# HGRN2's values and K turned by VectorE and transfers, and retention's states weighted ahead of a sum by ones, from the third unit on

## The chip, the cores and the metric

One core of a Trainium2 chip runs one launch of the kernel. The metric is device time in microseconds (us), median of three executions. The profile is of one execution. Its engines are written PE (TensorE matmuls), PEld (TensorE weight loads), DVE (VectorE), ACT (ScalarE), POOL (GpSimd) and SP (the queue from which nearly all transfers are issued).

## The reference, cut to what matters

One decoder layer works on 16 meta tokens, 256 prompt tokens and 8 sample tokens (one new token of each of 8 sequences with a past state):

```python
x = layer_norm(ALPHA * x + 0.5 * swiglu_1(x))
x = layer_norm(ALPHA * x + mixer(x))
x = layer_norm(ALPHA * x + 0.5 * swiglu_2(x))

# mixer: ten projections of x, 2048 wide each; retention (8 heads of 256), HGRN2 (16 heads of 128)
o = inner @ v + (q * decay) @ S                   # of one sequence, chunk by chunk
S_new = decay_to_the_end * S + k_decayed.T @ v
# the 8 samples: one token each, on a state of their own (8 x heads x 256 x 256, 8 x 16 x 128 x 128)
y = sigmoid(a_r) * norm(o_ret) * silu(g_r) + sigmoid(a_h) * rms_norm(o_hg) * silu(g_h)
out = y @ w_out
```

Two sums of it are touched. The HGRN2 state needs `K.T @ v` over the tokens, so both K and the values must stand with tokens on the partitions, while the projections leave them with features there. And a retention sample's output is its query times its new state, a sum over 256 features: 8 samples and 2 halves of 128 features for each head.

## The kernel before, in words

Activations lie with features on partitions and 280 tokens (or 264, without the meta tokens) in the free dimension. Every weight block of 128 x 128 is split into an upper and a lower part (`whi`, `wlo`), every activation into `xh` and `xl`, and a block costs three matmuls (whi with xh, whi with xl, wlo with xh), all on line 218. Weights come in loads of 8 blocks (512 KB): SP issues the transfer into `raw`, ACT casts it to `whi` (line 188), DVE subtracts to `wlo` (line 189), and 24 matmuls use them. Each of the three tiles has three buffers, so a new `raw` transfer waits until the `wlo` of three loads before is made, and a new `whi` until the 24 matmuls of three loads before are done.

The middle stage handles eight units; a unit is one retention head and two HGRN2 heads. A unit has six projection groups (f, q_h, i_h, q_r, k_r, v_r) and then four gate groups of the unit before it (g_r with a_r, g_h with a_h, twice), ten groups of 16 steps; a step is 6 matmuls, two blocks. So a unit is 960 dense matmuls, or 40 weight loads. The mixers `mix_hg` and `mix_ret` are generators. `evacuate`, called when a group's sums are complete, starts them: `mix_hg` at the end of i_h, `mix_ret` at the end of v_r. After each step `pump` counts the generators down, and each `yield n` lets n steps pass before the next piece is put into the program. PE's order is that of the program, and the matmuls of the mixers stand between dense ones at steps that the yields set. The other engines and SP run queues in an order which a scheduler wrote from priorities and its own estimates when the program was built; each then waits at the head of its queue for semaphores. The first two units differ in some pauses; the last six are alike, and this text calls them the steady units.

What the change touches:

- `mix_hg`, values. `i_h` ends; ACT copies both heads from PSUM to `v` (lines 667 and 668). For each head PE turns two blocks of 128 tokens (`pt<-ident,v`, line 875), in the second head's step also `ends`, the meta tokens and the last 16 columns (line 878), and ACT copies the result to `vt` (tile `vth`).
- `mix_hg`, K. When K is scaled, `turned(h)` turns two blocks of each head on PE (`ptk<-ident,K`, line 982), one head at a time, and ACT copies them to `kth`. `pst` (lines 1022 and 1024) multiplies them with `vth` to the states `Sh`; `pq` (line 1039) is the samples' product; `po` the outputs.
- `mix_ret`, states. `load` brings the sample states (`smr`, four tiles of 128 x 4 x 256: two groups `e` of four samples, two halves `c` of the features), ACT scales them by the decay (line 1192), DVE adds key times value (line 1198, the value spread over partitions as `vbr`), SP writes them out (`out_srs`, line 1202). Later `pqr` (line 1211) multiplies 16 pieces, `smr[e][c][:, j, :]`, by `qdr`, a tile of zeros in which each sample's query stands in one column, 32 columns a piece, summed in PSUM.
- POOL has small copies only, some of which do nothing but hold a transfer back until a tile is free (lines 769 and 773).

Of the kernel before, what the change touches and what calls it, by code (L numbers as in the profile page):

```python
# [13 lines left out]
AF = mybir.ActivationFunctionType  # L14
# [4 lines left out]
P = 128  # L19
# [109 lines left out]
def trunk(ctx: ExitStack, tc: tile.TileContext, A, O):  # L129
# [417 lines left out]
    with tc.tile_pool(name="yp", bufs=1) as yp:  # L547
# [7 lines left out]
        with tc.tile_pool(name="mp", bufs=1) as mp:  # L555
# [35 lines left out]
            nc.gpsimd.memset(qdh, 0.0)  # L591
            nc.gpsimd.memset(qdr, 0.0)
            qdh_at = [qdh.rearrange("p a c -> p (a c)")[:, 256 * h :] for h in range(2)]
            qdr_at = [qdr.rearrange("p a c -> p (a c)")[:, 2 * ALONE * c :] for c in range(2)]
            vsm = tmp("vsm", (P, P))
            vt2 = tmp("vt2", (P, 2, P))
# [51 lines left out]
            def evacuate(n, c0, c1, o0, o1, b0, b1):  # L648
# [12 lines left out]
                        mul_biased(q[:, j, :], o, b, q[:, j, :])  # L661
                    st["q"] = q
                elif n == "i_h":
                    v = st.pop("i_h", None)
                    if v is None:
                        v = tmp("v", (P, 2, T))
                        nc.scalar.copy(v[:, 0, :], o0)
                        nc.scalar.copy(v[:, 1, :], o1)

                    start(mix_hg(c0 // 2, st["f"], st["k"], st["q"], v), {0: 20, 2: 46}.get(c0, 4))  # L670
                elif n in ("q_r", "k_r"):
                    sc, w, x0 = (1.0, TL, NMETA) if n == "q_r" else (KSC, T, 0)
                    r = tmp(n, (P, 2, w))
# [8 lines left out]
                elif n == "v_r":  # L682
                    v = tmp("v", (P, 2, T))
                    nc.scalar.copy(v[:, 0, :], o0)
                    nc.scalar.copy(v[:, 1, :], o1)
                    start(mix_ret(c0 // 2, st["q_r"], st["k_r"], v), 24 if c0 == 2 else 3)
                elif n in ("g_r", "g_h"):
                    sg = tmp("gs", (P, TL), bufs=2)
                    t = tmp("gt", (P, TL), bufs=2)
                    nc.scalar.activation(sg, o0, AF.Sigmoid)  # L690
                    mul(t, sg, o0)
                    sa = tmp("gs", (P, TL), bufs=2)
                    nc.scalar.activation(sa, o1, AF.Sigmoid)
                    mul(t, t, sa)
                    u, e = divmod(c0, 2)
                    while u not in (done_r if n == "g_r" else done_h):
                        pump()
                    if n == "g_r":
                        y = tmp("y", (P, TL))
                        mul(y, t, on_r[u][:, e, :])  # L700
                        st["y"] = y
                    else:
                        y = st["y"]
                        nc.vector.scalar_tensor_tensor(
                            out=t, in0=t, scalar=ngt[:, c0 : c0 + 1], in1=on_h[u][:, e, :], op0=ALU.mult, op1=ALU.mult)

                        ys[c0] = y if c0 < EARLY else yp.tile([P, TL], F32, tag=f"y{c0}", name=f"y{c0}")
                        add(ys[c0], y, t)
                        if c0 < EARLY:
                            split(yh[c0], yl[c0], y)  # L710

            NB2 = LP - 2 * P
            BLOCKS = ((0, P), (P, P), (2 * P, T - 2 * P))

# [6 lines left out]
            def upper_upper_lower(out, x, at=0):  # L721
                n = x.shape[0]
                nc.scalar.copy(out[:n], x)
                nc.scalar.copy(out[32 : 32 + n], x)
                sub(out[64 : 64 + n], x, out[at : at + n].bitcast(F32))

            def rows_out(src, width, tag):

# [17 lines left out]
            def mix_hg(u, f, k, q, v):  # L746

                calm = 2
                ends = tmp("ends", (P, 2, 2, NMETA))
                nc.gpsimd.tensor_copy(ends[:, :, 0, :], v[:, :, :NMETA])  # L750
                nc.gpsimd.tensor_copy(ends[:, :, 1, :], v[:, :, T - NMETA :])
# [114 lines left out]

                join(1)
                Q1 = side_by_side(1)
                vt = tmp("vth", (P, 2, 2, P))
                vrow = []  # L870
                for h in range(2):

                    pt = mx_bank("pt")
                    for b in range(2):
                        nc.tensor.transpose(pt[:, b * P : (b + 1) * P], v[:, h, NMETA + b * P : NMETA + (b + 1) * P], ident)
                    x = pt[:64, 2 * P : 3 * P]
                    if h:
                        nc.tensor.transpose(x, ends.rearrange("p c a t -> p (c a t)"), ident)
                    nc.scalar.copy(vt[:, h], pt[:, : 2 * P].rearrange("p (b f) -> p b f", b=2))
# [205 lines left out]
            def mix_ret(u, q, k, v):  # L1085
# [18 lines left out]
                for c in range(2):  # L1104
# [84 lines left out]
                for e in range(2):  # L1189
# [11 lines left out]
                    for c in range(2):  # L1201
                        nc.sync.dma_start(O["srs"][u, c, :, 4 * e : 4 * e + 4, :], ss[c])
                    yield 1 if e else 10 if u == 0 else 6
                yield (11 if u == 0 else 15) + 2 * calm
                pq = mx_bank("pqr")
                scores(pq[:, 256:], 2)
                for e in range(2):
                    for c in range(2):
                        for j in range(4):
                            b = 4 * e + j  # L1210
                            nc.tensor.matmul(  # L1211
                                pq[32 * j : 32 * j + 32, :256], qdr_at[c][:, 32 * b : 32 * b + 32],
                                sms[2 * e + c][:, j, :], start=e + c == 0, stop=e + c == 2, tile_position=(0, 32 * j))
# [163 lines left out]
```

## Time and profile before

| what | value |
|---|---|
| time, median of 3 | 2566.66 us (2566.41 to 2567.9) |
| the profiled execution, first to last instruction | 2563.9 us |
| what lies around the span, against the median | 2.8 us |
| busy: PE, PEld | 2553.4, 2534.4 us |
| busy: DVE, ACT, POOL | 1702.8, 1392.2, 57.0 us |
| granted TensorE clock | 1.000 |
| data moved | 536.26 MB, mean 209 GB/s |
| middle stage, a steady unit | 126.3 us |

The page gives the profiled execution's span, and no time of its own besides. An engine counts as busy while one of its instructions runs. Matmuls overlap, so a row of 280 ns for one matmul is not its cost: in the timeline the dense matmuls start 0.119 us apart with 280 columns and 0.1125 us apart with 264. What a piece of other PE work costs is read from how far it pushes the next dense matmul back.

### The profile page before, as it was taken

The numbers are of one execution on the slowest core, as the hardware profiler recorded it, in microseconds if no ns is written. First come the engines' busy times: TensorE is split into PE (matmuls) and PEld (weight loads), VectorE is DVE, ScalarE is ACT, GpSimd is POOL, SyncE is SP. The second block draws the span as 40 slices with busy tenths as digits, with TensorE's granted clock in tenths as the row PEclk, the third lists the DMA queues.
The fourth block names the chain that finished last, engine by engine and source line by source line (L and its number), as shares of the span: only waits on it lengthen the run. The fifth ranks groups of instructions, "written<-read, shape, count | busy, mean of one in ns | idle before, by whom it ended". The sixth has DMA issues, their size and how long they took to land.

```text
span 2563.9 us, 56275 instructions
## 1 busy us (share of the span) xinstructions
PE 2553.4 (100%) x23424; PEld 2534.4 (99%) x23424; DVE 1702.8 (66%) x2827; ACT 1392.2 (54%) x2186; POOL 57.0 (2%) x152
## 2 busy tenths in 40 slices
PE   9999999999999999999999999999999999999999
PEld 9999999999999999999999999999999999999998
DVE  6444544475569878777777777777885555556555
ACT  5444444444456767767676666675564444444443
POOL 0000000000000000000000000000000000000000
PEclk9999999999999999999999999999999999999999
DMA  7555555555555876767676767675556565565554
GB/s 244 183 187 183 187 182 184 186 182 186 184 201 180 287 265 232 264 214 260 212 264 215 259 223 255 224 239 188 196 190 197 194 197 195 194 196 195 195 195 149
DMA packets 156897, 536.26 MB, mean 209 GB/s; under 512 B 17952, under 2 KB 25952, under 8 KB 156640
## 3 DMA queue, kind: packets, MB, share of 16 engines
q1 hardware_dynamic: 156352, 532.37, 62.0%
q8 instruction: 183, 3.00, 0.5%
q14 instruction: 74, 0.61, 0.1%
q10 hardware_dynamic: 288, 0.29, 0.0%
HBM read 501.99 MB, written 30.61 MB: 208 GB/s over the span
## 4 chain that ended last, share of the span: by engine, by line
PE 96%; DVE 2%; ACT 0%; issue 0%; DMA 0%; SPq 0%; ACTq 0%; DVEq 0%
PE up L218 36%; PE dn L218 19%; PE pj_i_h L218 3%; PE pj_g_r L218 3%; PE pj_q_h L218 3%; PE pj_g_h L218 3%; PE pj_a_r L218 3%; PE pj_a_h L218 3%; PE pj_f L218 3%; PE pj_q_r L218 3%; PE pj_k_r L218 3%; PE wo L218 3%; PE pj_v_r L218 3%; DVE wlo L189 1%; PE pqr L1211 1%; PE psr L1168 0%
## 5 line engine op out<-in xcount | busy, mean ns | idle before, releaser
L189 DVE TENSOR_TENSOR wlo<-raw,whi 128x1024 fp32r<-128x1024 f32 (+1 forms) x869 | 1062.2, 1223 | 740.7 <-ACT whi L188 737.3
L188 ACT CAST whi<-raw 128x1024 fp32r<-128x1024 f32 (+1 forms) x870 | 905.7, 1042 | 909.2 <-PE up L218 411.0
L218 PE MATMUL up<-xh,whi 128*128 128x280 f32 (+1 forms) x2624 | 725.6, 280 | 0.6 <-ACT whi L188 0.6
L218 PE MATMUL up<-xh,wlo 128*128 128x280 f32 (+1 forms) x2624 | 725.8, 280 | 0.4 <-DVE wlo L189 0.3
L218 PE MATMUL up<-xl,whi 128*128 128x280 f32 (+1 forms) x2624 | 725.4, 279 | 0.0
L218 PEld LDWEIGHTS up<-xh,wlo 128*128 128x128 f32 x2624 | 492.6, 189 | 1.0 <-DVE wlo L189 1.0
L218 PEld LDWEIGHTS up<-xh,whi 128*128 128x128 f32 x2624 | 492.6, 189 | 0.8 <-ACT whi L188 0.8
L218 PEld LDWEIGHTS up<-xl,whi 128*128 128x128 f32 x2624 | 492.6, 189 | 0.0
L218 PE MATMUL dn<-hh,whi 128*128 128x280 f32 (+1 forms) x1376 | 384.7, 280 | 0.0
L218 PE MATMUL dn<-hh,wlo 128*128 128x280 f32 (+1 forms) x1376 | 384.3, 279 | 0.0
L218 PE MATMUL dn<-hl,whi 128*128 128x280 f32 (+1 forms) x1376 | 384.3, 279 | 0.0
L218 PEld LDWEIGHTS dn<-hh,whi 128*128 128x128 f32 x1376 | 260.1, 189 | 0.1
L218 PEld LDWEIGHTS dn<-hl,whi 128*128 128x128 f32 x1376 | 260.1, 189 | 0.1
L218 PEld LDWEIGHTS dn<-hh,wlo 128*128 128x128 f32 x1376 | 260.1, 189 | 0.0
L218 PE MATMUL pj_k_r<-xh,whi 128*128 128x280 f32 x256 | 74.2, 290 | 0.0
L218 PE MATMUL pj_g_r<-xh,whi 128*128 128x264 f32 x256 | 74.0, 289 | 0.0
L218 PE MATMUL pj_v_r<-xh,whi 128*128 128x280 f32 x256 | 73.8, 288 | 0.0
L218 PE MATMUL pj_v_r<-xh,wlo 128*128 128x280 f32 x256 | 72.4, 283 | 0.3 <-DVE wlo L189 0.3
L218 PE MATMUL pj_g_h<-xh,whi 128*128 128x264 f32 x256 | 72.7, 284 | 0.0
L218 PE MATMUL pj_k_r<-xh,wlo 128*128 128x280 f32 x256 | 72.4, 283 | 0.0
L218 PE MATMUL pj_v_r<-xl,whi 128*128 128x280 f32 x256 | 72.3, 283 | 0.0
L218 PE MATMUL pj_k_r<-xl,whi 128*128 128x280 f32 x256 | 72.3, 283 | 0.0
(421 smaller groups left out, 5263.4 us busy)
## 6 DMA issues: line engine op xcount, KB each, us to landing
raw<-in_w_up SPq DMA_DIRECT2D x343, 512.0 KB, 4.1
raw<-in_w_in SPq DMA_DIRECT2D x320, 512.0 KB, 4.3
raw<-in_w_dn SPq DMA_DIRECT2D x172, 512.0 KB, 3.5
smr<-in_sr SPq DMA_DIRECT2D x32, 512.0 KB, 5.0
out_srs<-smr SPq DMA_DIRECT2D x32, 512.0 KB, 6.7
raw<-in_w_out SPq DMA_DIRECT2D x32, 512.0 KB, 3.9
vbr<-vrd SPq DMA_DIRECT2D x32, 256.0 KB, 4.1
smh<-in_sg SPq DMA_DIRECT2D x16, 512.0 KB, 5.2
```

The lines of the kernel that those rows point to most:

```text
L188: nc.scalar.copy(hi[:, j:jn, :], raw[:, j:jn, :])
L189: nc.vector.tensor_tensor(out=lo[:, j0:j1, :], in0=raw[:, j0:j1, :], in1=hi[:, j0:j1, :].bitcast(F32), op=ALU.subtract)
L218: nc.tensor.matmul(o, w, t, start=start, stop=stop)
L1211: nc.tensor.matmul(pq[32 * j : 32 * j + 32, :256], qdr_at[c][:, 32 * b : 32 * b + 32], sms[2 * e + c][:, j, :], start=e + c == 0, stop=e + ...
```

## The change

For units with u > 1 alone:

- Values: DVE turns blocks of 32 x 32 straight from PSUM (two instructions on 128 x 256, into the tile `v`), and 16 transfers of SP put the blocks in their places in `vth` (`turned_over`, one transfer each second step). ACT copies only the end columns. PE keeps the turn of `ends`.
- K: one DVE instruction turns 128 x 512 into the tile `k` (which is no longer needed then), and 16 transfers put the blocks into the tile `f`, from which `pst` reads. POOL's copies that hold back transfers now read `k` and `f`.
- Pauses of `mix_hg`: 30 steps instead of 5 ahead of `pst`, 42 instead of 45 between `pst` and `pq`.
- Retention's samples: after the states went out they are weighted in place by the queries. POOL (for e = 0) or ACT (for e = 1) multiplies the half c = 0 by its query column, DVE multiplies the half c = 1 by its own and adds: 4 + 4 + 8 instructions on 128 x 256. A copy from the latest gate tile (`st["seen"]`) stands ahead of the queries' copy on POOL. `pqr` then needs 8 pieces instead of 16, with ones in a column in place of the queries.
- Pauses of `mix_ret`: a start after 5 steps instead of 3, and 23 + 16 steps instead of 19 ahead of `pqr`.

```diff
             qdh_at = [qdh.rearrange("p a c -> p (a c)")[:, 256 * h :] for h in range(2)]
+            one = qdr[:, 0, :64].rearrange("p (e m) -> p e m", e=2)
+            late_q = qdr[:, 1, : 2 * NS].rearrange("p (c b) -> p c b", c=2)
...
                 elif n == "i_h":
-                    v = st.pop("i_h", None)
-                    if v is None:
+                    v, vt = st.pop("i_h", None), tmp("vth", TURNED)
+                    ends = tmp("ends", (P, 2, 2, NMETA))
+                    if c0 > 2:
+                        z = squared(tmp("v", (P, 2, T)))
+                        for j, o in enumerate((o0, o1)):
+                            nc.vector.transpose(z[:, j].rearrange("p b t -> p (b t)"), o[:, NMETA:LP])
+                            nc.scalar.copy(ends[:, j, 0, :], o[:, :NMETA])
+                            nc.scalar.copy(ends[:, j, 1, :], o[:, T - NMETA : T])
+                        turned_over(vt, z, 2)
+                    elif v is None:
...
-                    start(mix_ret(c0 // 2, st["q_r"], st["k_r"], v), 24 if c0 == 2 else 3)
+                    start(mix_ret(c0 // 2, st["q_r"], st["k_r"], v), {0: 3, 2: 24}.get(c0, 5))
...
                     nc.scalar.activation(sa, o1, AF.Sigmoid)
+                    st["seen"] = sa
...
+            TURNED = (P, 2, 2, P)
+            squared = lambda x: x.rearrange("p h t -> p (h t)")[:, : 4 * P].rearrange("p (h b t) -> p h b t", h=2, b=2)
...
+            def turned_over(out, z, pause):
+
+                def transfers():
+                    for i in range(0, P, 32):
+                        for j in range(0, P, 32):
+                            nc.sync.dma_start(out[j : j + 32, :, :, i : i + 32], z[i : i + 32, :, :, j : j + 32])
+                            yield pause
+
+                start(transfers(), 1)
...
-                    nc.gpsimd.tensor_copy(sms[h][:, 0, :1], kts[0][:, 0, :1] if h else acc[:, 15:16])
+                    nc.gpsimd.tensor_copy(sms[h][:, 0, :1], (kts[0] if u < 2 else k)[:, 0, :1] if h else acc[:, 15:16])
...
-                    nc.gpsimd.tensor_copy(vbs[h][:, 0, :1], kts[1][:, 0, :1] if h else acc[:, 2 * P + 15 : 2 * P + 16])
+                    n = 32 if h and u > 1 else P
+                    nc.gpsimd.tensor_copy(vbs[h][:n, 0, :1], kts[1][:n, 0, :1] if h else acc[:, 2 * P + 15 : 2 * P + 16])
...
-                    pt = mx_bank("pt")
-                    for b in range(2):
-                        nc.tensor.transpose(pt[:, b * P : (b + 1) * P], v[:, h, NMETA + b * P : NMETA + (b + 1) * P], ident)
+                    if u < 2 or h:
+                        pt = mx_bank("pt")
+                    if u < 2:
+                        for b in range(2):
+                            nc.tensor.transpose(pt[:, b * P : (b + 1) * P], v[:, h, NMETA + b * P : NMETA + (b + 1) * P], ident)
...
-                kts = []
+                kts = [squared(f)[:, h] for h in range(2)] if u > 1 else []
 
                 def turned(h):
+                    if u > 1:
+                        if h == 0:
+                            z = squared(k)
+                            nc.vector.transpose(z.rearrange("p h b t -> p h (b t)"), K[:, :, NMETA:])
+                            turned_over(squared(f), z, 2)
+                        return
...
                     samples(1)
-                    yield 4 if u == 0 else 5
+                    yield 4 if u == 0 else 30
...
-                yield (8, 11, 45)[min(u, 2)]
+                yield (8, 11, 42)[min(u, 2)]
...
-                alone(qdr, q)
+                if u < 2:
+                    alone(qdr, q)
...
-                yield (11 if u == 0 else 15) + 2 * calm
+                yield (11, 15, 13)[min(u, 2)] + 2 * calm if u < 2 else 23
+                if u == 2:
+                    nc.gpsimd.memset(qdr[:, 0, :64], 0.0)
+                    for e in range(2):
+                        nc.gpsimd.memset(one[:, e, e : e + 1], 1.0)
+                if u > 1:
+                    nc.gpsimd.tensor_copy(late_q[:, 0, :1], st["seen"][:, :1])
+                    nc.gpsimd.tensor_copy(late_q, q[:, :, SEQ:])
+                    for e in range(2):
+                        s0, s1 = sms[2 * e : 2 * e + 2]
+                        for b in range(4):
+                            g = [late_q[:, c, 4 * e + b : 4 * e + b + 1] for c in range(2)]
+                            if e:
+                                nc.scalar.activation(s0[:, b, :], s0[:, b, :], AF.Copy, scale=g[0])
+                            else:
+                                nc.gpsimd.tensor_scalar(out=s0[:, b, :], in0=s0[:, b, :], scalar1=g[0], scalar2=None, op0=ALU.mult)
+                            nc.vector.scalar_tensor_tensor(
+                                out=s0[:, b, :], in0=s1[:, b, :], scalar=g[1], in1=s0[:, b, :], op0=ALU.mult, op1=ALU.add)
+                    yield 16
...
                 for e in range(2):
-                    for c in range(2):
+                    for c in range(2 if u < 2 else 1):
                         for j in range(4):
                             b = 4 * e + j
                             nc.tensor.matmul(
-                                pq[32 * j : 32 * j + 32, :256], qdr_at[c][:, 32 * b : 32 * b + 32],
-                                sms[2 * e + c][:, j, :], start=e + c == 0, stop=e + c == 2, tile_position=(0, 32 * j))
+                                pq[32 * j : 32 * j + 32, :256], qdr_at[c][:, 32 * b : 32 * b + 32] if u < 2 else one[:, e, :],
+                                sms[2 * e + c][:, j, :], start=e + c == 0, stop=e + c == 2 if u < 2 else e == 1, tile_position=(0, 32 * j))
```

How the queues move is shown for the fourth unit (u = 3), as one of the six. Names without a number have one buffer name for all rotations.

On PE, where the samples' products stand, with a dense row on either side. Before, in the third gate group (g_r with a_r):

```order
L218 MATMUL pj_a_r_15214<-xl_10_9276,whi_15276 128x264
L218 MATMUL pj_a_r_15214<-xh_10_9275,wlo_15277 128x264
L1039 MATMUL pq<-smh,qdh 32x128 x16
L1141 MATMUL pqr<-q_r,k_r 16x16 x2
L1211 MATMUL pqr<-smr,qdr 32x256 x16
L218 MATMUL pj_g_r_15213<-xh_11_9279,whi_15276 128x264
```

And now, in the f group of the next unit:

```order
L218 MATMUL pj_f_15542<-xl_0_9235,whi_15544 128x280
L218 MATMUL pj_f_15542<-xh_0_9235,wlo_15545 128x280
L1070 MATMUL pq<-smh,qdh 32x128 x16
L1173 MATMUL pqr<-q_r,k_r 16x16 x2
L1261 MATMUL pqr<-smr,qdr 32x256 x8
L218 MATMUL pj_f_15541<-xh_1_9239,whi_15544 128x280
```

The two products moved together by 22 steps (132 dense matmuls), and `pqr` has 8 pieces instead of 16.

On DVE, at the same two places (`wlo` is the weights' lower part, `gt` and `y` gate work). Before:

```order
L189 TENSOR_TENSOR wlo_15277<-raw_15275,whi_15276 128x8x128
L240 TENSOR_TENSOR gt<-gt,gs 128x264
L704 SCALAR_TENSOR_TENSOR gt<-gt,ngt,on_h 128x264
L252 TENSOR_TENSOR y_15211<-y,gt 128x264
L189 TENSOR_TENSOR wlo_15355<-raw_15353,whi_15354 128x8x128
L189 TENSOR_TENSOR wlo_15396<-raw_15394,whi_15395 128x8x128
L240 TENSOR_TENSOR scr_8637<-pqr,dtab 16x16
```

Now, ahead of `pqr`:

```order
L189 TENSOR_TENSOR wlo_15473<-raw_15471,whi_15472 128x8x128
L240 TENSOR_TENSOR gt<-gt,gs 128x264
L1252 SCALAR_TENSOR_TENSOR smr<-smr,qdr 128x256
L240 TENSOR_TENSOR y<-gt,on_r 128x264
L1252 SCALAR_TENSOR_TENSOR smr<-smr,qdr 128x256 x3
L189 TENSOR_TENSOR wlo_15503<-raw_15501,whi_15502 128x8x128
L1252 SCALAR_TENSOR_TENSOR smr<-smr,qdr 128x256 x4
L189 TENSOR_TENSOR wlo_15545<-raw_15543,whi_15544 128x8x128
```

The eight weightings stand in the queue between the lower parts of weight loads, the first four ahead of `wlo_15503`.

On SP, around the transfer of the retention values' rows (`vrd`). Before:

```order
L1002 DMA out_sgs<-smh 128x1024
L1030 DMA out_sgp<-Sh 128x128 x2
L185 DMA raw_15101<-in_w_in 128x1024
L730 DMA vrd<-vt_8636 8x256
L185 DMA raw_15143<-in_w_in 128x1024
L1156 DMA vbr<-vrd 128x512 x2
```

Now:

```order
L185 DMA raw_15130<-in_w_in 128x1024
L744 DMA f<-k 32x4x32 x2
L185 DMA raw_15178<-in_w_in 128x1024
L744 DMA f<-k 32x4x32 x5
L185 DMA raw_15220<-in_w_in 128x1024
L744 DMA f<-k 32x4x32
L752 DMA vrd<-vt_8636 8x256
L185 DMA raw_15262<-in_w_in 128x1024
L1188 DMA vbr<-vrd 128x512 x2
```

The last eight of K's 16 transfers stand among the weight loads just ahead of `vrd`, and the transfer of the new states (`out_sgp`) stands fifteen rows behind `vrd`.

More of the change, by code (lines that the diff above doesn't have):

```diff
@@ L668, in evacuate @@
                         nc.scalar.copy(v[:, 1, :], o1)
-                    start(mix_hg(c0 // 2, st["f"], st["k"], st["q"], v), {0: 20, 2: 46}.get(c0, 4))
+                    start(mix_hg(c0 // 2, st["f"], st["k"], st["q"], v, ends, vt), {0: 20, 2: 46}.get(c0, 4))
                 elif n in ("q_r", "k_r"):
@@ L744, in sample_columns, with mix_hg @@
                     po[:, 3 * P :].rearrange("p (j c) -> p c j", c=32)[:, : 2 * n, :].rearrange("p (h e) j -> p h e j", e=2))
-            def mix_hg(u, f, k, q, v):
+            def mix_hg(u, f, k, q, v, ends, vt):
                 calm = 2
-                ends = tmp("ends", (P, 2, 2, NMETA))
-                nc.gpsimd.tensor_copy(ends[:, :, 0, :], v[:, :, :NMETA])
-                nc.gpsimd.tensor_copy(ends[:, :, 1, :], v[:, :, T - NMETA :])
+                if u < 2:
+                    nc.gpsimd.tensor_copy(ends[:, :, 0, :], v[:, :, :NMETA])
+                    nc.gpsimd.tensor_copy(ends[:, :, 1, :], v[:, :, T - NMETA :])
                 Q = tmp("Q", (P, 2, SEQ))
@@ L868, in mix_hg @@
                 Q1 = side_by_side(1)
-                vt = tmp("vth", (P, 2, 2, P))
                 vrow = []
                 for h in range(2):
-                    pt = mx_bank("pt")
-                    for b in range(2):
-                        nc.tensor.transpose(pt[:, b * P : (b + 1) * P], v[:, h, NMETA + b * P : NMETA + (b + 1) * P], ident)
-                    x = pt[:64, 2 * P : 3 * P]
+                    if u < 2 or h:
[3 more added lines that the diff above has]
+                            nc.tensor.transpose(pt[:, b * P : (b + 1) * P], v[:, h, NMETA + b * P : NMETA + (b + 1) * P], ident)
                     if h:
+                        x = pt[:64, 2 * P : 3 * P]
                         nc.tensor.transpose(x, ends.rearrange("p c a t -> p (c a t)"), ident)
-                    nc.scalar.copy(vt[:, h], pt[:, : 2 * P].rearrange("p (b f) -> p b f", b=2))
+                    if u < 2:
+                        nc.scalar.copy(vt[:, h], pt[:, : 2 * P].rearrange("p (b f) -> p b f", b=2))
                     if h:
@@ L1132, in mix_ret @@
                     yield 2
-                alone(qdr, q)
+                if u < 2:
+                    alone(qdr, q)
                 vts = [vt[:, 0], vt[:, 1], vs2]
```

## The prediction

> **What bounds the kernel.** I read the page's engine lines first, then its chain that ended last, PE's waits, and last one steady unit by its window.
>
> ```profile
> span 2563.9 us, 56275 instructions
> PE 2553.4 (100%) x23424; PEld 2534.4 (99%) x23424; DVE 1702.8 (66%) x2827; ACT 1392.2 (54%) x2186; POOL 57.0 (2%) x152
> PE 96%; DVE 2%; ACT 0%; issue 0%; DMA 0%; SPq 0%; ACTq 0%; DVEq 0%
> ...
> PE pw L515 <- DVE eps_h L163: 1.0, 1, 1.0
> ...
> 1122.00:1248.30 126.30, 126.30 (x1276) 124.63 (x1275) 98.54 (x195) 84.80 (x157) 6.19 (x15) 1.00 0.70 239
> ```
>
> PE is busy for 2553.4 of 2563.9 us, and the longest of its waits, the first row of that view, is 1.0 us in total. In the last row, a steady unit, PE is busy for all of 126.30 us at a clock of 1.00, DVE for 98.54, ACT for 84.80, and the transfers for a share of 0.70. So the end moves by what PE's queue loses, unless PE must wait somewhere it does not wait now. The median lies 2.8 us above the profiled span; nothing around the span is touched, so I subtract from the median.
>
> **What PE loses.** A busy time counts overlaps twice, so I take starts. With nothing between, dense matmuls start 0.1125 us apart (264 columns) or 0.119 (280).
>
> ```profile
> 1121.97 0.28 PE L218 MATMUL pj_q_r<-xh,wlo 128*128 128x264 f32 x1
> 1122.09 0.38 PE L875 MATMUL pt<-ident,v 128*128 128x128 f32 x2
> 1122.42 0.28 PE L218 MATMUL pj_q_r<-xl,whi 128*128 128x264 f32 x1
> ...
> 1122.87 0.28 PE L218 MATMUL pj_q_r<-xh,wlo 128*128 128x264 f32 x1
> 1122.98 0.38 PE L875 MATMUL pt<-ident,v 128*128 128x128 f32 x2
> 1123.20 0.27 PE L878 MATMUL pt<-ident,ends 128*64 128x128 f32 x1
> 1123.42 0.28 PE L218 MATMUL pj_q_r<-xl,whi 128*128 128x264 f32 x1
> ...
> 1140.10 0.28 PE L218 MATMUL pj_k_r<-xh,wlo 128*128 128x280 f32 x1
> 1140.22 0.38 PE L982 MATMUL ptk<-ident,K 128*128 128x128 f32 x2
> 1140.56 0.28 PE L218 MATMUL pj_k_r<-xl,whi 128*128 128x280 f32 x1
> ...
> 1148.41 0.28 PE L218 MATMUL pj_v_r<-xh,wlo 128*128 128x280 f32 x1
> 1148.53 0.27 PE L988 MATMUL ptm<-ident,meta 128*64 128x128 f32 x1
> 1148.76 0.28 PE L218 MATMUL pj_v_r<-xl,whi 128*128 128x280 f32 x1
> ...
> 1191.60 0.42 PE L1211 MATMUL pqr<-smr,qdr 128*32 128x256 f32 x3
> 1191.65 1.89 PE L1211 MATMUL pqr<-smr,qdr 128*32 128x256 f32 x29
> 1193.47 0.38 PE L218 MATMUL pj_g_r<-xh,whi 128*128 128x264 f32 x1
> ```
>
> - Values, first head: from 1121.97 to the second dense start behind it, 1122.42, are 0.45 us instead of 2 x 0.1125, so the two turns cost 0.225 us. They go whole.
> - Values, second head: 1122.87 to 1123.42 is 0.55, a cost of 0.325. `ends` stays; a lone turn of the same size (`ptm`) costs 1148.76 - 1148.41 - 2 x 0.119 = 0.11. Gain 0.215.
> - K: 1140.56 - 1140.10 - 2 x 0.119 = 0.222 for one head, 0.444 for both, gone.
> - `pqr`: 1191.60 to 1193.47 is 1.87 us for 32 passes of 16 pieces. The new pieces have the same shape, so half goes: 0.93.
>
> Sum 0.225 + 0.215 + 0.444 + 0.93 = 1.81 us a unit, 10.9 us for six. All else on PE only changes its place; `pq` and `pqr` move together. In the last unit the norm's sums come behind fewer steps, since the gate there pumps four steps without dense work between; they join one piece. I allow 0.5 us lost there.
>
> **What the other engines get.** Per unit, DVE gets eight instructions like its state updates, two turns on 256 columns from PSUM and one on 512. No row shows a DVE turn; the bounds are an arithmetic instruction of that width (0.42 and 0.69 us) and three times that. I take 0.42 and 0.69, since all DVE rows of 256 columns lie near 0.42.
>
> ```profile
> L1198 DVE SCALAR_TENSOR_TENSOR smr<-vbr,k_r,smr 128x256 f32<-128x256 f32 x40 | 16.9, 480 | 6.3 <-ACT smr L1192 6.3
> L1027 DVE SCALAR_TENSOR_TENSOR Sh<-Sh,T,pst 128x128 f32<-128x128 f32 x20 | 5.6, 343 | 0.2
> L240 DVE TENSOR_TENSOR Q<-q,f 128x512 f32<-128x512 f32 x5 | 3.5, 691 | 0.2
> L240 DVE TENSOR_TENSOR Q<-Q,f 128x256 f32<-128x256 f32 x5 | 2.1, 420 | 0.0
> ```
>
> That is 8 x 0.48 + 2 x 0.42 + 0.69 = 5.4 us on 98.54, or 104 of 124.5; even at three times for the turns, 107. ACT loses six copies out of PSUM and gets four tiny ones and four scalings, near nothing in sum. As totals these are hidden behind PE; at nothing they count only while weight loads stay ahead of PE, and that is decided in two stretches.
>
> **The lead of the weights.** A load's last step is `wlo` on DVE. Counting 24 matmuls a load, the `wlo` of 1170.10 serves the matmul at 1175.25, and the `wlo` of 1187.26 the one at 1188.75.
>
> ```profile
> 1170.10 1.21 DVE L189 TENSOR_TENSOR wlo<-raw,whi 128x1024 fp32r<-128x1024 f32 x1
> 1175.25 0.28 PE L218 MATMUL pj_g_h<-xh,wlo 128*128 128x264 f32 x1
> ...
> 1187.26 1.22 DVE L189 TENSOR_TENSOR wlo<-raw,whi 128x1024 fp32r<-128x1024 f32 x1
> 1188.75 0.28 PE L218 MATMUL pj_g_r<-xh,wlo 128*128 128x264 f32 x1
> ...
> 1182.99 0.39 ACT L690 ACTIVATE gs<-pj_g_h 128x264 f32<-128x264 f32 x1 [0.60 <-PE pj_g_h L218]
> 1185.35 1.05 ACT L188 CAST whi<-raw 128x1024 fp32r<-128x1024 f32 x1 [1.97 <-DMA raw<-in_w_in]
> 1186.31 0.38 ACT L693 ACTIVATE gs<-pj_a_h 128x264 f32<-128x264 f32 x1
> ...
> 1198.47 1.23 DVE L189 TENSOR_TENSOR wlo<-raw,whi 128x1024 fp32r<-128x1024 f32 x1 [0.81 <-ACT whi L188]
> ```
>
> The lead falls from 1175.25 - 1171.31 = 3.94 us to 1188.75 - 1188.48 = 0.27 us over five loads, while retention's states are read, scaled, updated and written; ACT waits there for `raw` itself. Then the 3 us of `pq` and `pqr` at 1190.6 rebuild the lead, since PE takes no weights in them. The change does three things here. It puts `pst` (1.1 us of PE without weights) into this dip, which helps by 1.1 us, with its four `Sh` updates on DVE (1.4 us), which may hurt as much if DVE is what is late; by the waits shown it is the transfers. It moves the rebuilding 22 steps, or 132 x 0.1125 = 15 us, later. And it puts the weighting into those 15 us. From 1187.26 to 1198.47 four loads came, 2.80 us each, while PE needs 24 x 0.1125 = 2.70: the supply nearly keeps pace, and the next unit's two state loads (1 MB), which are among the transfers then, now come only after `pqr`. I therefore expect the lead to stay near 1 us and grow a little.
>
> **The weighting.** Let G be the end of the third gate group. ACT then has a sigmoid, a cast and a sigmoid (0.4 + 1.05 + 0.4, some 2.1 us with hand-overs) if `raw` is there; as the rows at 1182.99 and 1186.31 show, 3.7 if it isn't. POOL's two small copies and four scalings follow.
>
> ```profile
> 1148.36 0.23 POOL L1103 COPY tails<-k_r 128x48 f32<-128x48 f32 x1 [4.01 <-DVE k_r L680]
> 1158.97 1.22 DVE L189 TENSOR_TENSOR wlo<-raw,whi 128x1024 fp32r<-128x1024 f32 x1
> 1159.15 1.11 POOL L1103 COPY tails<-v 128x48 f32<-128x48 f32 x1 [8.90 <-ACT v L685]
> L592 POOL MEMSET qdr<- 128x516 f32 x1 | 0.5, 532 | 0.0
> ```
>
> A POOL scaling on 256 columns stands in no row. Between 0.23 us for 48 columns and 0.53 for 516 it is 0.4 to 0.5 by its size; the copy at 1159.15 took 1.11 and ended 0.07 us behind a `wlo` that ran beside it, so 1.7 (0.45 + 1.22) is the upper end. I take 0.45, since in the new queue DVE waits at the first weighting and runs no `wlo` against the following ones. The chain: G + 2.1, copies 0.4, four scalings 1.8, DVE's last weighting 0.5, `wlo` 1.2: the load is made at G + 6.0. PE uses it 74 matmuls after G, at G + 8.3. With each scaling waiting for DVE's weighting before it (0.48) it is 7.9, still in time. `pqr` stands 102 matmuls and `pq` after G, at 12.5; the four weightings of e = 1 end by 9.9. So the weighting costs PE nothing, with 0.4 to 2.3 us to spare.
>
> **Transfers.** 32 more a unit, 16 KB each, 0.5 MB on some 30 MB.
>
> ```profile
> raw<-in_w_in SPq DMA_DIRECT2D x320, 512.0 KB, 4.3
> out_srs<-smr SPq DMA_DIRECT2D x32, 512.0 KB, 6.7
> out_srp<-sro SPq DMA_DIRECT2D x16, 128.0 KB, 2.3
> ```
>
> A landing takes between 2.3 and 6.7 us here. K's last transfer is put in 14 steps ahead of `pst`, 84 x 0.1125 = 9.5 us, and `psc` and `psr` (2.8 us) lie between too, so `pst` does not wait. SP's queue gets 32 issues; a `raw` behind five of them starts perhaps 1 to 2 us later, where the lead is 4 us. Price 0 to 1 us a unit, I take 0.
>
> **Rivals.**
> 1. The dip goes under: the `Sh` updates and K's last eight transfers fall into it and outweigh the 1.1 us of `pst`. PE then waits 0.5 to 1.5 us a unit, 3 to 9 in all: 2559 to 2565. For it speaks the lead of 0.27; against it, that ACT waits for transfers there, not for DVE.
> 2. The weighting comes late because POOL and DVE hold each other up, as at 1159.15. With `raw` late by 1.6 us and one `wlo` in POOL's way (1.2) the load is made at G + 8.8, and PE waits 0.5 us a unit: 2559.5. With a `wlo` in the way of each of the four scalings (4 x 1.22) it is made at G + 10.9, PE waits 2.6 us a unit, and the time is 2572. For it speaks that row, against it the queue, in which DVE waits at the first weighting with no `wlo` running. The Trainium skill's page "SBUF — State Buffer" says under "Who interferes with whom" that a VectorE instruction with two inputs in SBUF and a GpSimd instruction that reads SBUF exclude each other for their whole length. The row at 1159.15 agrees; by that rule alone, with POOL losing each time, the sum would be 2572 instead of 2556.5.
> 3. Slower: the lead is not rebuilt for 15 us, and supply stays as slow as in the dip. There the lead lost 3.7 us over five loads, 0.73 a load; over 5.5 more loads PE would wait 4 us a unit, 24 us in all: 2580. It decides from a wait of 2.7 us a unit, (10.9 + 5.1) / 6. Against it stands the pace of 2.80 us from 1187.26 on.
> 4. K lands late and `pst` waits, with dense work behind it: 1 us a unit, 2562. It needs a landing over 12 us.
>
> **How the numbers follow.** 2566.66 - 10.9 + 0.5 = 2556.3, and I add 0.2 for starts that shift: 2556.5 (2554.5 to 2559.5 as the case's own range). This case has 0.66; rival 1 has 0.13, rival 2 has 0.08, rival 3 has 0.10, rival 4 has 0.03. Measurement tells 0.2% (5.1 us) from no change, so faster means under 2561.5 and slower over 2571.8. Faster takes the first case and half of rivals 1 and 2 (0.105): 0.77; their other half and rival 4, 0.13, are the same; slower is rival 3, 0.10. The range 2554.5 to 2565 leaves out rival 3 and the top of rival 2.
>
> **What would show it.** PE's rows `pt<-ident,v`, `ptk` and half of `pqr` gone in six units, a steady unit of 124.5 us, and still no wait of PE on `wlo`, `whi` or `pst` in them. A POOL scaling near 0.45 us, a turn on DVE near 0.42. A wait of PE for `wlo` just behind the weighting would show rival 2, one at the states' writes rival 1, several in a row rival 3. The prediction is wrong if the unit is over 125.5 us.

## The result and the profile after

The changed kernel takes 2598.6 us (2596.08 to 2600.25) against 2566.66: a ratio of 1.0124, 95% interval 1.0109 to 1.0138. It is slower by 32 us where 10 us of gain were forecast. The page's engine lines and chain, PE's waits, and the same steady unit (u = 3, the same 960 dense matmuls as in the window shown of before):

```profile
span 2594.3 us, 56368 instructions
PE 2559.6 (99%) x23280; PEld 2535.1 (98%) x23280; DVE 1728.4 (67%) x2887; ACT 1387.2 (53%) x2196; POOL 77.0 (3%) x179
PE 85%; DVE 5%; DMA 5%; ACT 3%; issue 1%; POOL 1%; SPq 0%; DVEq 0%; ACTq 0%; POOLq 0%
...
PE pj_g_h L218 <- DVE wlo L189: 14.8, 10, 2.3
PE pj_g_r L218 <- DVE wlo L189: 6.3, 6, 1.9
PE pt L1147 <- POOL tails L1134: 2.4, 4, 0.9
...
1128.96:1261.77 132.81, 128.10 (x1252) 125.42 (x1251) 103.05 (x205) 84.16 (x159) 9.54 (x18) 0.99 0.70 232
```

The chain no longer runs through PE alone, PE waits for `wlo` in both gate halves, and the unit takes 132.8 us instead of 126.3. The saving on PE itself is there: `ptk` and the values' turns are gone from six units, and `pqr` takes 1.0 us instead of 1.87 (from its first piece to the next dense matmul):

```profile
1220.82 0.42 PE L1261 MATMUL pqr<-smr,qdr 128*32 128x256 f32 x3
1220.84 0.18 PE L1173 MATMUL pqr<-q_r,k_r 128*16 128x16 f32 x1
1220.86 1.03 PE L1261 MATMUL pqr<-smr,qdr 128*32 128x256 f32 x13
1221.82 0.39 PE L218 MATMUL pj_f<-xh,whi 128*128 128x280 f32 x1
```

Between the profiled executions (2594.3 and 2563.9 us) some 41 us were lost beside a gain of 10. To see where, I took the starts of neighbouring dense matmuls with no other PE work between them, and summed what they exceed 0.1125 or 0.119 us by, over the six units. "Dip" is the 600th to 900th dense matmul of a unit, counted from its f group (the states are read, scaled, updated and written there); "weighting" the 900th to 1040th. An excess over 0.13 us is a wait; one of 0.095 to 0.112 us a matmul that took twice its spacing, called slow here. Most slow ones are single, right behind a wait or behind a piece of other work, at a granted clock of 1.00 (as at 1187.5 us of the change); in the change three stretches of 15 in a row, 1.6 us each, ran at a clock near 0.5 (last section). These sums are of the profiled execution, the times are medians. The last column is ACT's time at the head of its queue waiting for the second half of the states (row `smr <- DMA smr<-in_sr` of its waits).

| kernel | median us | dip: waits, slow | weighting: waits, slow | ACT for `in_sr` |
|---|---|---|---|---|
| before | 2566.7 | 0, 0.6 | 0, 0 | 7.4 |
| after | 2598.6 | 14.2, 6.2 | 13.3, 3.2 | 31.7 |
| e3 pauses only | 2579.1 | 8.0, 1.9 | 0.3, 0.8 | 22.3 |
| e9 start only | 2577.2 | 5.4, 1.4 | 0, 0 | 21.0 |
| e10 pauses, old start | 2569.1 | 0.5, 0.4 | 0, 0.6 | 7.7 |
| e16 after, old start | 2590.3 | 2.2, 1.0 | 16.0, 6.0 | 19.8 |
| e2 weighting only | 2588.8 | 7.9, 2.7 | 14.1, 3.5 | 23.2 |
| e6 after, weighting on ACT | 2585.1 | 15.4, 4.9 | 1.9, 1.6 | 32.9 |
| e13 as e2, on ACT, old start | 2565.7 | 1.7, 0.2 | 1.8, 1.5 | 5.0 |
| e1 turns only | 2573.1 | 2.8, 1.7 | 0, 0 | 21.2 |
| e7 values only | 2565.6 | 1.1, 0.9 | 0, 0 | 8.5 |
| e8 K only | 2568.1 | 0.8, 1.0 | 0, 0 | 19.3 |

### The profile page after: what moved, and what is told of

The parts are those of the page before. It is cut to its first block, busy times and chain, and to the rows that moved or that the text cites. A ratio compares the mean times of both kernels' runs of the same rounds, so it can differ in the third digit from the quotient of the medians.

```text
span 2594.3 us, 56368 instructions
## 1 busy us (share of the span) xinstructions
PE 2559.6 (99%) x23280; PEld 2535.1 (98%) x23280; DVE 1728.4 (67%) x2887; ACT 1387.2 (53%) x2196; POOL 77.0 (3%) x179
## 4 chain that ended last, share of the span: by engine, by line
PE 85%; DVE 5%; DMA 5%; ACT 3%; issue 1%; POOL 1%; SPq 0%; DVEq 0%; ACTq 0%; POOLq 0%
PE up L218 36%; PE dn L218 18%; PE pj_i_h L218 3%; PE pj_q_h L218 3%; PE pj_q_r L218 3%; PE wo L218 3%; PE pj_f L218 3%; DMA raw<-in_w_in 3%; PE pj_k_r L218 2%; DVE wlo L189 2%; PE pj_g_r L218 2%; PE pj_a_r L218 2%; PE pj_v_r L218 2%; PE pj_g_h L218 1%; PE pj_a_h L218 1%
## 5 line engine op out<-in xcount | busy, mean ns | idle before, releaser
L218 PE MATMUL pj_g_h<-xh,wlo 128*128 128x264 f32 x256 | 72.9, 285 | 14.9 <-DVE wlo L189 14.8
L218 PE MATMUL pj_g_r<-xh,wlo 128*128 128x264 f32 x256 | 73.7, 288 | 7.1 <-DVE wlo L189 6.3
```

What stands on the lines that cost most here:

```text
L218: nc.tensor.matmul(o, w, t, start=start, stop=stop)
```

## The experiments

**The change taken apart.** Theory T: K's transfers make retention's rows late on SP, and the weighting comes late. Rival R: the products' move left the lead unbuilt.

e3, the kernel before with the changed pauses alone (ahead of retention's start, of `pst`, of `pq` and of `pqr`):

```diff
-                    start(mix_ret(c0 // 2, st["q_r"], st["k_r"], v), 24 if c0 == 2 else 3)
+                    start(mix_ret(c0 // 2, st["q_r"], st["k_r"], v), {0: 3, 2: 24}.get(c0, 5))
...
-                    yield 4 if u == 0 else 5
+                    yield 4 if u == 0 else 30
...
-                yield (8, 11, 45)[min(u, 2)]
+                yield (8, 11, 42)[min(u, 2)]
...
-                yield (11 if u == 0 else 15) + 2 * calm
+                yield (11, 15, 35)[min(u, 2)] + 2 * calm
```

> The kernel before with the changed pauses alone: pst 25 steps later, pq and pqr 22 steps later, nothing else. Theory T: no wait of PE over 1 us a unit, 2567 us (2565 to 2571). Rival R (the lead is not rebuilt because the products moved): at least half of the 30 us of waits returns, 2582 us or more.

Measured 2579.08 us, ratio 1.0051 (1.0036 to 1.0066): 12 us lost with no instruction changed. T missed; R's direction was right.

e1 is the change without its retention part (`pq` and `pqr` at their old place, 30 and 20 steps in `mix_hg`, retention's start after 3 steps as before), e2 the retention part alone (5 and 67 steps, start after 5), e4 the change with the turned blocks in rows of 512 B.

> The changed kernel without its retention part: values and K turned by VectorE and placed by 32 transfers a unit, pst 30 steps late; pq, pqr (16 pieces) and the retention pauses as before. Theory T (the transfers on SP's queue make retention's rows, and with them its state updates, late, and the second half of the loss is the weighting): PE gains 0.884 x 6 = 5.3 us, and keeps the waits of the changed kernel at the states' writes, 14.2 us, and the half-clock stretches behind them, 5.6 us: 2581 us (2575 to 2586). Rival R (the loss comes from the products' move 22 steps later, which leaves the lead unbuilt): 2561 us (2559 to 2566).

> The kernel before with the retention part alone: states weighted by POOL, ACT and DVE, pqr of 8 pieces, pq and pqr 22 steps later as in the change; values and K turned on PE, pst at its old place. Theory T: PE gains 0.93 x 6 = 5.6 us and loses, as in the changed kernel, 13.3 us of waits behind the weighting and 3.2 us at half clock, none at the states' writes: 2577 us (2570 to 2581). A rival in which the transfers alone carry the loss gives 2561 us; rival R (the move of the products) gives losses at the states' writes too, 2590 us or more.

e1 took 2573.11 us, 1.0025 (1.0014 to 1.0036); e2 2588.78 us, 1.009 (1.0075 to 1.0105). Neither lies in a forecast range: e1 is below T's and above R's, e2 above T's. Both parts lose, the weighting more, and e2 has waits in the dip without one added transfer, which T had excluded. In e1 the larger waits are new ones, for the tails of retention's values:

```profile
PE pt L1147 <- POOL tails L1134: 6.6, 7, 1.0
PE pt L1138 <- ACT v L693: 1.6, 3, 1.0
```

```diff
-    nc.sync.dma_start(out[j : j + 32, :, :, i : i + 32], z[i : i + 32, :, :, j : j + 32])
+    nc.sync.dma_start(out[32 * j : 32 * j + 32, i], z[32 * i : 32 * i + 32, j])
```

> The changed kernel with the turned blocks laid out so that each of the same 32 transfers a unit moves 32 rows of 512 B in place of 128 rows of 128 B. If the issue time on SP (0.6 to 0.8 us each, against 0.33 us of a weight load) goes by rows, it falls to about 0.35 us, retention's rows go out about 4 us earlier, and half of the dip's 20 us goes: 2588 us (2583 to 2594). If the number of issues, or their place in the queue, is what counts: 2598 us (2595 to 2601).

e4 took 2608.75 us, 1.0165 (1.0148 to 1.0182), slower than the change. Five issues of `f<-k` still took 3.73 us on SP (3.91 in the change), so the issue time does not go by rows. The time lies outside both ranges, though: operands with a stride of 16 B made the turns and `pst` slower (last section), and e4 says nothing more on the transfers.

**Is it the burst?** e5 leaves out most pieces of `pq` and `pqr` (`range(2)` and `range(NS)` cut to 1 and 4), at their old place, so the samples' outputs of those units are missing.

> The kernel before with most of the samples' products left out from the third unit on: 4 of the 16 pieces of pq a head pair and 4 of the 32 passes of pqr stay, so the samples' outputs of those units are not computed; all pauses, and all other work, as before. PE's burst of 3 us falls to about 0.6 us, a gain of 2.35 x 6 = 14 us if nothing else changes. Theory L (the burst is what rebuilds the weights' lead behind the states' writes, so moving it away costs what the kernel with the changed pauses alone lost): waits of 1.3 to 1.8 us a unit on wlo appear just behind the old place, and the time is 2562 us (2558 to 2566). Rival Q (moving the burst only reordered the queues of SP and DVE, the lead needs no burst): 2553 us (2551 to 2555).

Measured 2557.07 us, 0.996 (0.9946 to 0.9973). `pq` and `pqr` pushed dense work back by 0.97 us instead of 2.92, so PE saved 1.95 x 6 = 11.7 us, not the 14 I had worked out; 10.2 arrived. In the gate groups PE waited 1.6 us in all for `wlo`, where it waited for none before. The time lies between the two ranges; with 11.7 us in place of 14 the rival's 2553 becomes 2555.5 and L's 2562 becomes 2564.5. So the lead does without two thirds of the burst: L falls, and R with it.

**Which pause?** e9 changes one pause of the kernel before, retention's start from 3 to 5 steps (`pqr` keeps its place); e10 is e3 with that pause left at 3; e16 is the change with it put back to 3.

```diff
-                    start(mix_ret(c0 // 2, st["q_r"], st["k_r"], v), 24 if c0 == 2 else 3)
+                    start(mix_ret(c0 // 2, st["q_r"], st["k_r"], v), {0: 3, 2: 24}.get(c0, 5))
...
-                yield (11 if u == 0 else 15) + 2 * calm
+                yield (11, 15, 13)[min(u, 2)] + 2 * calm
```

> The kernel before with one pause changed: retention's mixer starts 5 steps behind v_r in place of 3, as in the change, and its pqr keeps its place. Theory S (the two steps, 1.35 us, push retention's row transfer vrd and the spreads vbr behind one more weight load on SP, and the state updates on DVE then stand waiting with wlo behind them; this is what made the kernel with the changed pauses alone slow): waits of 1.2 to 1.8 us a unit on wlo at the states' writes, 2575 us (2572 to 2579). Rival L (the product's move made it slow): no wait, 2567 us (2565 to 2569).

> The kernel before with all changed pauses but that one: pst 25 steps and pq and pqr 22 steps later, retention's mixer still starts 3 steps behind v_r. Theory S: vrd and vbr stand behind the same weight loads as before, the waits of the changed pauses go: 2568 us (2566 to 2571). Rival L (the products' move made it slow): 2577 us or more.

> The changed kernel with one pause put back: retention's mixer starts 3 steps behind v_r in place of 5, pqr keeps its place. Theory S (the start carries half of the dip's 20 us, K's transfers ahead of vrd the rest): the dip falls to 5 to 9 us, the waits on the tails grow by 4 to 6 us, the weighting is as in the change: 2589 us (2583 to 2594). Rival (K's transfers carry it all, the start nothing): 2598 us or more.

e9 took 2577.15 us, 1.0041 (1.0026 to 1.0056); e10 2569.14, 1.001 (1.0001 to 1.0019); e16 2590.25, 1.0089 (1.0076 to 1.0103). All three times lie in theory S's ranges, with details that do not: e9's waits were 0.9 us a unit instead of 1.2 to 1.8, and in e16 the dip fell further than the 5 to 9 us forecast. Two steps, 1.35 us, cost 10 us alone (7 to 14 by the interval), and moving `pst` and the products without them costs some 2.5. In the change they made 17 of the dip's 20 us (waits and slow matmuls of the table: 14.2 + 6.2 against 2.2 + 1.0). Of these 8 come back as time, since with the old start PE waits 6.5 us for the tails in place of 2.4, and 2.5 us for `v` in place of none, and 5.5 us more is lost at the weighting.

What the two steps do is seen in ACT's and DVE's waits, first of before, then of e10, e9 and after:

```profile
ACT smr L1192 <- DMA smr<-in_sr: 7.4, 10, 2.1
DVE smr L1198 <- DMA vbr<-vrd: 1.8, 2, 1.6
```

```profile
ACT smr L1192 <- DMA smr<-in_sr: 7.7, 9, 1.9
DVE smr L1198 <- DMA vbr<-vrd: 4.0, 5, 1.4
```

```profile
ACT smr L1192 <- DMA smr<-in_sr: 21.0, 13, 3.4
DVE smr L1198 <- DMA vbr<-vrd: 5.7, 7, 1.2
```

```profile
ACT smr L1224 <- DMA smr<-in_sr: 31.7, 14, 6.4
DVE smr L1230 <- DMA vbr<-vrd: 26.9, 14, 2.8
```

The rows of after in the dip of u = 3 (ACT, then DVE) show who stands behind them:

```profile
1181.09 1.03 ACT L188 CAST whi<-raw 128x1024 fp32r<-128x1024 f32 x1
1186.85 1.15 ACT L1224 ACTIVATE smr<-smr,sro 128x1024 f32<-128x1024 f32 x1 [4.73 <-DMA smr<-in_sr]
1187.90 0.41 ACT L1056 COPY Sh<-pst 128x128 f32<-128x128 f32 x2
1188.20 1.06 ACT L188 CAST whi<-raw 128x1024 fp32r<-128x1024 f32 x1
```

```profile
1180.48 0.41 DVE L240 TENSOR_TENSOR gt<-gt,gs 128x264 f32<-128x264 f32 x1
1182.97 0.48 DVE L1230 SCALAR_TENSOR_TENSOR smr<-vbr,k_r,smr 128x256 f32<-128x256 f32 x1 [2.07 <-DMA vbr<-vrd]
1183.37 0.43 DVE L240 TENSOR_TENSOR y<-gt,on_r 128x264 f32<-128x264 f32 x1
1183.81 0.41 DVE L255 TENSOR_TENSOR vs<-vt,vs 24x256 fp32r<-24x256 f32 x1
1184.24 2.07 DVE L1230 SCALAR_TENSOR_TENSOR smr<-vbr,k_r,smr 128x256 f32<-128x256 f32 x5
1186.22 1.22 DVE L189 TENSOR_TENSOR wlo<-raw,whi 128x1024 fp32r<-128x1024 f32 x1
```

The cast of the second load stands behind a scaling that waited 4.7 us for its states; the `wlo` of the first, cast by 1182.12, starts at 1186.22 because updates that waited for `vbr` stand ahead of it. The `raw` transfer of the third load after waits for such a `wlo` (SP issues it at 1187.47, that `wlo` ended at 1187.44), so the lateness goes round. That the start causes the loss is shown; that ACT's wait is the link that costs is read from the traces only, and it is not enough alone: e8 has 19.3 us of it and loses nearly nothing. More buffers for the states were not tried.

The start also changes an order. In each of the six units of the kernels that start after 5 steps (after, e2, e3, e4, e6, e9, e11) ACT's queue has the gate's two sigmoids, with a cast between them, ahead of the first scaling; in those that start after 3 steps the first two scalings stand ahead of both. ACT's rows before, then of e9:

```profile
1171.39 2.19 ACT L1192 ACTIVATE smr<-smr,gam 128x1024 f32<-128x1024 f32 x2 [1.29 <-POOL gam L1174]
1173.48 0.35 ACT L1170 COPY sro<-psr 128x256 f32<-128x256 f32 x1
1173.73 0.39 ACT L690 ACTIVATE gs<-pj_g_r 128x264 f32<-128x264 f32 x1
```

```profile
1173.80 0.39 ACT L690 ACTIVATE gs<-pj_g_r 128x264 f32<-128x264 f32 x1
1174.09 1.04 ACT L188 CAST whi<-raw 128x1024 fp32r<-128x1024 f32 x1
1175.02 0.39 ACT L693 ACTIVATE gs<-pj_a_r 128x264 f32<-128x264 f32 x1
1175.30 1.15 ACT L1192 ACTIVATE smr<-smr,gam 128x1024 f32<-128x1024 f32 x1
```

So the 10 us are the price of the pause with the queues as the scheduler rewrote them. No run has the later start with the old order, and which of the two costs stays open.

Theory S also said how: `vrd` stands one weight load later on SP. e11 is the change, and e15 is e1, with `vrd` issued as soon as its source is made and put, with `vbr`, ahead of K's transfers.

> The changed kernel with vrd issued as soon as its source is made and vrd and vbr put ahead of K's waiting transfers on SP; nothing else. They then stand one weight load earlier than in the change, and still one later than before it. Theory S: of the dip's 20 us about half goes: 2589 us (2583 to 2594). Rival (SP's time or the transfers' load on the DMA engines is what counts, not the place of vrd): 2598 us (2595 to 2601).

> The kernel with both turns alone (2573 us), with vrd issued as soon as its source is made and vrd and vbr put ahead of K's transfers, so that they stand behind the same weight loads as before the change. Theory S: its waits on wlo at the states' writes (2.8 us and 1.2 us at half clock) go, those of pt on the tails (6.6 us) and on v (1.6 us), which come from PE overtaking ACT, stay: 2569.5 us (2566 to 2572). Rival (vrd's place among the transfers does not matter): 2573 us.

e11 took 2597.91 us, 1.0123 (1.0106 to 1.014), no gain: the dip's waits fell from 14.2 to 9.1 us, and those at the weighting rose from 13.3 to 17.9. e15 took 2578.24, 1.0043 (1.003 to 1.0057), 5 us slower than e1, with 7.8 us of waits in the dip. e15 lies above both of its forecasts. So an earlier `vrd` does not bring the loss back. The traces agree: counted from the first gate matmul of u = 3, `vrd` is issued after 4.8 us before the change, 5.5 in e9, 12.6 in the change, and 12.4 in e16, whose dip loses 3.2 us. This part of S falls. And as e15 has the old start and the old order on ACT, the dip can lose in other ways too; which one it is there is not known.

**The weighting.** e6 gives POOL's part (two copies, four scalings) to ACT; e13 is e2 with that and the old start.

```diff
...
-    nc.gpsimd.tensor_scalar(out=s0[:, b, :], in0=s0[:, b, :], scalar1=g[0], scalar2=None, op0=ALU.mult)
+    nc.scalar.activation(s0[:, b, :], s0[:, b, :], AF.Copy, scale=g[0])
```

> The changed kernel with POOL's part of the weighting (the hold-back copy, the queries' copy and four scalings a unit) moved to ACT, whose scaling of this size takes 0.50 us against POOL's 0.94. Theory P (the weighting is late because POOL's chain takes 4.9 us from its first copy to its last scaling where 2.2 were priced, and wlo stands behind it on DVE): the load behind the weighting is made 2.5 us earlier, its waits of 13.3 us and 3.2 us at half clock fall to 3 us or less, and the time is 2586 us (2581 to 2590). Rival (the weighting's place is what is wrong: raw is late there anyway and DVE has 4.5 us more to do, so the engine does not matter): 2597 us (2594 to 2601).

> The kernel before with the retention part alone, its weighting on ACT and DVE without POOL, retention's mixer started at 3 steps as before, pq and pqr 22 steps later. Theory S and P: pqr's half gives 5.6 us, the later products cost the 2.5 us of the kernel with the later pauses and the old start, the weighting on ACT 3 us: 2566 us (2562 to 2570). Rival (the weighting costs its place on DVE whatever the engine): 2574 us or more.

e6 took 2585.12 us, 1.007 (1.0056 to 1.0084), 13.5 us faster than the change and as theory P had it, and the waits at the weighting fell from 13.3 to 1.9. e13 took 2565.67, 0.9994 (0.9985 to 1.0003): repaired, the retention part no longer costs time, but 4 of the 5 us that it saves on PE (0.86 x 6) are given back.

**The turns one by one**, e7 the values' part of the change alone, e8 K's part alone (`pst` 25 steps later, products at their place).

> The kernel before with the values' part of the change alone: two turns on DVE and 16 transfers a unit in place of four turns on PE and two copies on ACT; K, the pauses and retention as before. PE gains 0.44 x 6 = 2.6 us. The 16 transfers stand where the lead of the weights is 3 to 6 us. Theory T: nothing waits, 2564.2 us (2563 to 2566). Rival (16 more issues on SP make weight loads late there too): no gain or a loss, 2567 us or more.

> The kernel before with K's part of the change alone: one turn on DVE and 16 transfers a unit, pst 25 steps later with the products at their old place; values turned on PE, retention as before. PE gains 0.444 x 6 = 2.7 us. Theory T (K's transfers stand ahead of retention's rows on SP, and POOL's hold-back copy waits for them with the tails' copy behind it): nearly all waits of the kernel with both turns stay, 3 us on wlo, 1 us at half clock and 6 us on the tails: 2572 us (2569 to 2575). Rival (values and K cost the same): 2570 us and the values alone as much.

e7 took 2565.6 us, 0.9995 (0.9986 to 1.0004); e8 2568.07, 1.0003 (0.9994 to 1.0011). Each alone is no change in time (e8 stands below both its forecasts), but against the 2.6 and 2.7 us that PE saves e7 gives back 1.0 and e8 3.5; together (e1) they cost 6 us. e1's 8.2 us of waits for `tails` and `v` are 1.9 in e8, and in e7 0.9 as in the kernel before. A reading that no run tests: each part lets PE reach the end of v_r earlier, and in e1 it gets there ahead of ACT, which still scales HGRN2's states.

**Repairs.** e12 is the change with e6's and e11's edits and a start at 4 steps; e14 is e13 with the values' part.

> The changed kernel with three edits: POOL's part of the weighting on ACT, vrd and vbr put ahead of K's transfers, and retention's mixer started at 4 steps, so that vrd stands behind the same weight load as before the change. Theory S and P together: the weighting's waits are gone as on ACT (2585 us), and of the 20 us at the states' writes 14 or more go: 2569 us (2562 to 2576). Rival (the waits only move elsewhere): 2585 us (2580 to 2590).

> The same with the values' part of the change added (two turns on DVE and 16 transfers a unit; K still on PE, pst at its old place). The values alone gave 1.6 us of the 2.6 that PE saves: 2564 us (2560 to 2568), which would be the fastest of all. Rival (both parts together lose, as both turns did): 2570 us or more.

e12 took 2579.1 us, 1.005 (1.0035 to 1.0065), with 7.7 us of waits in the dip and 4.9 for the tails; e14 2566.75, 1.0 (0.9991 to 1.0009). e12 stands above its range, e14 within it but without the gain. No version that computes everything beats the kernel before by more than the measurement can tell.

## Why the prediction was wrong

- **PE's gain** held: 0.44 us for the values, 0.444 for K and 0.86 for `pqr` (0.93 forecast) is 1.75 a unit against 1.81.
- **DVE's turns** held, at 0.425 and 0.700 us against 0.42 and 0.69:

```profile
L671 DVE STREAM_TRANSPOSE v<-pj_i_h 128x256 f32<-128x256 f32 x12 | 4.6, 425 | 0.0
L1005 DVE STREAM_TRANSPOSE k<-K 128x512 f32<-128x512 f32 x6 | 4.2, 700 | 0.0
```

- **The lead of the weights** is where the step failed. It named three things that the change does in the dip, `pst`, the products and the weighting, and left out the fourth pause in the same diff, retention's start two steps later. That had no price; alone it costs 10 us (e9), and in the change it makes 17 of the 20 us lost in the dip (e16). The lead, forecast to stay near 1 us, was gone: PE waited 14.2 us there. Rival 3 had the size of such a loss (4 us a unit), and the wrong reason: without the later start the moved products cost 2.5 us (e10), and the lead hardly needs the burst (e5).
- **The weighting** is a term mis-sized. The third gate group of u = 3 is done at G = 1203.6, where the first matmul of the fourth starts. The rows:

```profile
1208.01 0.95 POOL L1242 COPY qdr<-gs 128x1 f32<-128x1 f32 x1 [23.73 <-ACT gs L702]
1209.02 0.29 POOL L1243 COPY qdr<-q_r 128x16 f32<-128x16 f32 x1
1209.41 3.68 POOL L1251 TENSOR_SCALAR smr<-smr,qdr 128x256 f32<-128x256 f32 x4
...
1213.13 0.48 DVE L1252 SCALAR_TENSOR_TENSOR smr<-smr,qdr 128x256 f32<-128x256 f32 x1 [0.21 <-POOL smr L1251]
1213.53 1.22 DVE L189 TENSOR_TENSOR wlo<-raw,whi 128x1024 fp32r<-128x1024 f32 x1
1214.67 1.67 DVE L1252 SCALAR_TENSOR_TENSOR smr<-smr,qdr 128x256 f32<-128x256 f32 x4
1214.81 0.38 PE L218 MATMUL pj_g_h<-xh,wlo 128*128 128x264 f32 x1 [2.27 <-DVE wlo L189]
```

  The load is made at G + 11.1, not G + 6.0. The gate's last sigmoid ended at G + 4.4 instead of 2.1 (the cast ahead of it waited 2.2 us for `raw`), the copies took 1.4 us instead of 0.4, and a scaling 0.92 instead of 0.45. This is rival 2's second case (G + 10.9) by another cause: the first of the four scalings took 0.92 us with nothing on DVE beside it, and the others, with DVE busy beside them, 0.92 to 0.98. The rule of the Trainium skill that rival 2 named ("SBUF — State Buffer", "Who interferes with whom") would hold DVE up for the whole of a scaling; the weightings beside POOL took 0.69 us instead of 0.48, so here the trace does not agree. For the copy at 1208.01 it does: it ended at 1208.96, 0.04 us behind a `wlo`.
- **Transfers at nothing**: neither turn alone makes the kernel slower, but K's gives back all of its gain, and both together (e1) bring 8.2 us of waits for `tails` and `v`. That PE overtakes ACT there is the reading above. `pst` did not wait for K, as forecast; its longest wait was 0.4 us, for `km`.

## What to carry to other kernels

Where several in-order queues feed each other, give every pause in a diff a price of its own, the smallest too: look at which waiting instruction it moves past what stands behind it. A lead of 0.3 us means that the order in the queues is tight, not that it holds. An engine that is idle 97% of the time still sets the pace where another queue waits at its head for it, and its price is a row of the same operation and size, or else the upper bound.

## What was not expected of the hardware

A wait of PE can cost more than itself. Behind the 2.43 us of waiting before 1214.81 the dense matmuls started 0.22 us apart for 3.3 us, at a granted clock of 0.52 (the column ahead of the DMA share):

```profile
1212.00:1215.40 3.40, 1.09 (x7) 0.89 (x8) 2.99 (x6) 1.89 (x2) 1.09 (x2) 1.00 0.20 52
1215.40:1218.80 3.40, 3.40 (x19) 3.40 (x18) 3.20 (x5) 0.06 (x1) 0.00 (x0) 0.52 0.92 305
```

Of the six waits of 2.0 to 2.5 us in the change three were followed by this, at 1.6 us each. The Trainium skill's page "TensorE: Matmul & The Clock Gate" (Part 1) states half rate after an idle window of about 3.4 us that runs free of the kernel; here shorter waits did it, and not every time.

Operands with a stride of 16 B were dear: in e4 a DVE turn of 256 columns took 662 ns instead of 425, and `pst` pushed dense work back by 2.08 us instead of 1.03.

```profile
L742 DVE STREAM_TRANSPOSE v<-pj_i_h 128x256 f32<-128x256 f32 x12 | 7.0, 662 | 0.0
```
